# A streaming-encoder block on one core: the low part of every second v tile of the last FFN, made by ScalarE and an accumulating transfer

## The chip, the cores and the metric

The kernel runs on one core of one Trainium2 chip. A core has a matrix engine (TensorE, in the profile PE, with its weight loads as PEld), a vector engine (VectorE, DVE), an engine for functions of single elements (ScalarE, ACT), a general one (GpSimd, POOL) and a queue that issues transfers (SyncE, SP). Each works through its own list of instructions in order; they meet through semaphores. 16 DMA engines move data between the device's memory (HBM) and the on-chip memory (SBUF); TensorE adds up its products in the eight banks of PSUM. The metric is the device time of one execution in microseconds (us), lower is better.

## The reference

One layer over 256 rows of 2048 numbers: a half-step FFN, a mixer (mLSTM heads beside recurrent channels), and a second half-step FFN, each with a normalisation that is shifted and scaled by a condition c. The change lies in the second FFN:

```python
def _swiglu(u, w13, w2):
    g, v = jnp.split(u @ w13, 2, axis=-1)
    return (jax.nn.silu(g) * v) @ w2
...
        y = _swiglu(modulate(x, 2), ffn2_w13[l], ffn2_w2[l])
        x = _layer_norm(ALPHA * x + FFN_WEIGHT * gate[:, 2, None, :] * y, ln_g[l, 2], ln_b[l, 2])
```

`u` is 256 x 2048, `w13` is 2048 x 11264 (5632 columns of g, 5632 of v), `w2` is 5632 x 2048; everything is float32.

## The kernel before

**Two parts for every number.** The products run in a float32 form of TensorE (`F32R`, fp32r in the profile) that keeps fewer digits than float32. So each weight tile is split into a high part (the value, written as fp32r) and a low part (the value minus the high part), and the activations `u` likewise (`uh`, `ul`). A product is then three matmuls: activation high by weight high (L271), activation high by weight low (L272), activation low by weight high (L273). These are the three lines of `mov_t`; `mov_w` calls it once for each half of the 256 rows.

**A weight tile's way.** `load` takes a raw buffer, one of four, and lets SyncE fetch a tile of 128 x 2048 numbers, 1024 KB (L87). `split` takes a `hi` and a `lo` buffer, three of each in rotation; ScalarE writes `hi` (L97), then VectorE writes `lo` as raw minus hi (L99), which also releases the raw buffer. `load_w` is the two together. The four raw buffers also serve "ada" tiles: weights of the condition, which VectorE reduces beside the FFN's work at a fixed rate (`tick`, L191).

**The last FFN.** `ffn(2, ...)` has no `start`. Its 5632 inner columns are worked in 11 blocks of 512. `rows_block` computes one block: four g tiles (k = 0 to 3), each a fourth of the 2048 inner elements, into two banks (one for each half of the rows), then four v tiles into two others; then `swiglu` makes silu(g) * v. Block 0 is begun ahead of the FFN and goes through `met`; the other ten take the path shown. Their results are transposed by TensorE (`turn_one`, L685), after the g tiles k = 1 and 2 of the next block or within the w2 products, and split by ScalarE (hth, L687) and VectorE (htl, L688). After every two blocks, `g2` multiplies the 16 w2 tiles of the group before (rw, lw, hw in the profile; banks py). In the profile the g tiles of all FFNs are rfg, hfg and lfg, with the products fg, and the v tiles rfv, hfv and lfv, with the products fv. `closing` and `boundary` finish the last group and the normalisation.

**Order.** The program is written in order of use, and a planner places the instructions on their engines by a simulated timeline. The tiles' buffers rotate, so a cast (L97) can start once TensorE is done with the tile three places back in the rotation.

Of the kernel before, what the change touches and what calls it, by code (L numbers as in the profile page):

```python
# [11 lines left out]
F32 = mybir.dt.float32  # L12
F32R = mybir.dt.float32r
AF = mybir.ActivationFunctionType
ALU = mybir.AluOpType

P = 128
# [30 lines left out]
def block_kernel(ctx: ExitStack, tc: tile.TileContext, a: dict, out: bass.AP):  # L48
    nc = tc.nc
    cst = ctx.enter_context(tc.tile_pool(name="cst", bufs=1))  # L50
    big = ctx.enter_context(tc.tile_pool(name="big", bufs=1))
    wp = ctx.enter_context(tc.tile_pool(name="wp", bufs=1))
# [12 lines left out]
    def bank(name):  # L65
        return psp.tile([P, 512], F32, tag="ps", name=name)
# [4 lines left out]
    def raw_tile(name):  # L71
        n_raw[0] += wide[0]
        if wide[0] and n_raw[0] % 3 == 0:
            return slot(name)[:, 0:D]
        return wp.tile([P, 2048], F32, tag="raw", bufs=4, name=name)
# [7 lines left out]
    def load(src, name, into=None):  # L83

        tick()
        raw = raw_tile("r" + name)
        queue().dma_start(raw, src)  # L87
        return raw, name, into

    def split(tile, act, low):  # L90

        raw, name, into = tile
        hi, lo = into() if into else [wp.tile([P, 2048], F32R, tag=w, bufs=3, name=w[0] + name) for w in ("hi", "lo")]
        step = 512 if fine[0] else 2048
        cols = [slice(c, c + step) for c in range(0, 2048, step)]
        for w in cols:
            act.copy(cut(hi, w), like(raw[:, w], hi))  # L97
        for w in cols:
            low.tensor_sub(cut(lo, w), like(raw[:, w], lo), cut(hi, w).bitcast(F32))  # L99
        return hi, lo  # L100

    def load_w(src, name, into=None):

        return split(load(src, name, into), nc.scalar, nc.vector)

    def cut(t, w):

        return t[:, w] if len(t.shape) == 2 else t[:, w.start // P:w.stop // P, :]

    def like(ap, t):  # L110
        return ap if len(t.shape) == 2 else ap.rearrange("p (a b) -> p a b", b=P)
# [17 lines left out]
    def queue():  # L129

        return Q if wide[0] else nc.sync
# [38 lines left out]
    uh, ul = u2[:, :, 0, :], u2[:, :, 1, :]  # L170
# [28 lines left out]
    def tick():  # L199

        credit[0] += credit[1]
        while todo and credit[0] >= 1.0:
            credit[0] -= 1.0
            ada_tile(V if wide[0] else nc.vector)
# [59 lines left out]
    def mov_t(ps, hl, acth, actl, k0, t, first, last):  # L264

        hi, lo = hl
        tk = slice(t * P, (t + 1) * P)
        for j in range(4):
            w = slice(j * 512, (j + 1) * 512)
            o = like(ps, hi)  # L270
            nc.tensor.matmul(o, acth[:, k0 + j, tk], cut(hi, w), start=first and j == 0, stop=False)  # L271
            nc.tensor.matmul(o, acth[:, k0 + j, tk], cut(lo, w), start=False, stop=False)  # L272
            end = nc.tensor.matmul(o, actl[:, k0 + j, tk], cut(hi, w), start=False, stop=last and j == 3)  # L273
        return end
# [21 lines left out]
    def mov_w(pss, hl, acth, actl, k0, first, last):  # L296
        for t in range(NT):
            end = mov_t(pss[t], hl, acth, actl, k0, t, first, last)
        return end
# [30 lines left out]
    def boundary(s, ps, hls, order, mm, sts, following, gated=False):  # L330
# [152 lines left out]
        for k in ready:  # L483
            fw[k] = split(fw[k], nc.scalar, V)
# [132 lines left out]
    def met(passed, src, nm):  # L617

        _, ps, hl, raws = passed
        pss = [ps, bank(f"{nm}b1")]  # L620
        alone = [k for k in range(4) if k not in raws]
        for k in range(4):
            if k:
                hl = split((raws[k], f"{nm}b{k}", None), nc.scalar, nc.vector) if k in raws else load_w(src[k], f"{nm}b{k}")
            if k in alone:
                mov_t(pss[0], hl, uh, ul, k * 4, 0, not raws and k == 0, k == alone[-1])
            mov_t(pss[1], hl, uh, ul, k * 4, 1, k == 0, k == 3)
        return pss
# [4 lines left out]
    def ffn(s, w13, w2, start, following=None):  # L633
# [11 lines left out]
        def new_h(gi):  # L645
            hts[gi] = [slot(f"{w}{gi}", F32R)[:, 0:GRP * S].rearrange("p (a b) -> p a b", a=GRP) for w in ("hth", "htl")]

        def rows_block(b, passed=None):

            i = 8 * (b - b0)  # L650
            if passed:
                pg, pv = passed[0], met(passed, w13[4:8], f"fv{s}")
            else:
                pg = [bank(f"fg{s}{b}{t}") for t in range(NT)]
                for k in range(4):
                    end = mov_w(pg, load_w(w13[i + k], f"fg{s}_{b}{k}"), uh, ul, k * 4, k == 0, k == 3)
                    if k in (1, 2):
                        turn_one(end)
                pv = [bank(f"fv{s}{b}{t}") for t in range(NT)]
                for k in range(4):  # L660
                    mov_w(pv, load_w(w13[i + 4 + k], f"fv{s}_{b}{k}"), uh, ul, k * 4, k == 0, k == 3)
            if 4 * b // GRP not in hts:
                new_h(4 * b // GRP)
            for t in range(NT):
                swiglu(b, t, pg[t], pv[t])

        def swiglu(b, t, g, v):

            sg = sm.tile([P, 512], F32, tag="u", bufs=2, name=f"sg{s}{b}{t}")
            nc.scalar.activation(sg, g, AF.Silu)  # L670
            nc.vector.tensor_mul(sg, sg, v)
            to_turn.append((b, t, sg))

        def turn_one(end):

            if not to_turn:
                return
            b, t, sg = to_turn.pop(0)
            hth, htl = hts[4 * b // GRP]
            i = 4 * b % GRP  # L680
            tk = slice(t * P, (t + 1) * P)
            ps = bank(f"th{b}{t}")
            with tc.issue_after(end.ins):
                for j in range(4):
                    nc.tensor.transpose(ps[:, j * P:(j + 1) * P], sg[:, j * P:(j + 1) * P], ident)  # L685
            ps = ps.rearrange("p (a b) -> p a b", a=4)
            nc.scalar.copy(hth[:, i:i + 4, tk], ps)  # L687
            nc.vector.tensor_sub(htl[:, i:i + 4, tk], ps, hth[:, i:i + 4, tk].bitcast(F32))  # L688
            if to_make:
                swiglu(*to_make.pop(0))  # L690
# [152 lines left out]
        def g1(gi):  # L843
            grp = groups[gi]
            if start and gi == 2:
                new_h(gi)
                with tc.issue_after(evac[-1].ins):
                    nc.scalar.dma_start(bq, a["b_s"])
                    nc.scalar.dma_start(rgp, a["rgp"])
                to_make.extend((b, t, part[b, 0][t], part[b, 1][t]) for b in (4, 5) for t in range(NT))  # L850
                for t in range(NT):
                    swiglu(*to_make.pop(0))
                return
            if start and gi == 3:
                for t in range(NT):
                    nc.scalar.dma_start(x[:, t, :], a["x"][t * P:(t + 1) * P, :])
                scale_x()
            for b in range(grp[0] // 4, grp[-1] // 4 + 1):
                if b or start:
                    rows_block(b)  # L860
# [73 lines left out]
        if start is not None:  # L934
            ramp(start)
            credit[:] = 0.0, FFN1_RATE
            done = 2
            g2(0)
        else:
            credit[:] = -2.0, FFN2_RATE  # L940
            rows_block(0, nxt.pop())
# [482 lines left out]
```

## Time and profile before

| | |
|---|---|
| median of two runs | 1896.52 us (1895.68 to 1897.36) |
| the profiled execution, first to last instruction | 1893.8 us |
| TensorE, mean granted clock | 0.999 of full speed |
| weight tiles of 128 x 2048 in the last FFN's ten regular blocks | 80, of them 40 v tiles |
| one cast of such a tile on ScalarE (L97, hfv) | 1.91 us |
| one subtraction of such a tile on VectorE (L99, lfv) | 2.29 us |
| one load of such a tile, issue to landing (rfv) | 4.8 us |

How to read the lines that follow. A row of the timeline has the start in us from the span's start, the duration in us, the engine, the line of the kernel, the operation, and what it writes and reads; in brackets stands how long the engine had been idle, and what ended that. A row of a tile's view groups equal instructions: their count behind the x, then the least, median and largest duration in ns, then the first and last start. A row of windows has the stretch, its length, the busy time of each engine with its number of instructions, the clock granted to TensorE, the share of the DMA engines' time in use and the rate. "DMA to landing" is the time from the start of the issuing instruction to the data's arrival, least, median and largest.

### The profile page before, as it was taken

The numbers are of one execution on the slowest core, as the hardware profiler recorded it, in microseconds if no ns is written. First come the engines' busy times: TensorE is split into PE (matmuls) and PEld (weight loads), VectorE is DVE, ScalarE is ACT, GpSimd is POOL, SyncE is SP. The second block draws the span as 40 slices with busy tenths as digits, with TensorE's granted clock in tenths as the row PEclk, the third lists the DMA queues.
The fourth block names the chain that finished last, engine by engine and source line by source line (L and its number), as shares of the span: only waits on it lengthen the run. The fifth ranks groups of instructions, "written<-read, shape, count | busy, mean of one in ns | idle before, by whom it ended". The sixth has DMA issues, their size and how long they took to land.

```text
span 1893.8 us, 21255 instructions
## 1 busy us (share of the span) xinstructions
PE 1880.4 (99%) x8591; PEld 1544.5 (82%) x8591; DVE 1411.9 (75%) x1372; ACT 831.2 (44%) x790; POOL 41.3 (2%) x65
## 2 busy tenths in 40 slices
PE   9999999999999999999999999999999999999998
PEld 6788888888888888788888887888888888888886
DVE  6899998887887977798986877556555644545666
ACT  4443444533334335756643357343434334343341
POOL 0000000000000000000000121000000000000000
PEclk9999999999999999999999999999999999999999
DMA  9989889899899886477787663666676655555562
GB/s 378 416 355 360 311 315 374 336 354 351 344 362 356 333 316 252 170 289 269 274 320 269 215 248 128 242 257 248 239 258 242 227 196 193 184 200 202 198 222 89
DMA packets 74498, 515.87 MB, mean 272 GB/s; under 512 B 8688, under 2 KB 8864, under 8 KB 13472
## 3 DMA queue, kind: packets, MB, share of 16 engines
q1 hardware_dynamic: 72144, 507.54, 71.3%
q10 hardware_dynamic: 1728, 3.80, 0.6%
q0 software_dynamic: 528, 3.17, 0.4%
q8 instruction: 67, 1.10, 0.2%
q14 instruction: 31, 0.25, 0.0%
HBM read 512.36 MB, written 2.12 MB: 272 GB/s over the span
## 4 chain that ended last, share of the span: by engine, by line
PE 94%; DVE 3%; DMA 1%; ACT 1%; issue 1%; POOL 0%; POOLq 0%; DVEq 0%; SPq 0%; ACTq 0%
PE py L272 6%; PE py L271 6%; PE py L273 6%; PE fg L272 6%; PE fg L271 6%; PE fg L273 6%; PE fv L271 6%; PE fv L272 6%; PE fv L273 6%; PE pj L260 5%; PE pj L262 3%; PE tl L271 2%; PE tl L272 2%; PE tl L273 2%; PE rv L738 2%; PE rv L739 2%
## 5 line engine op out<-in xcount | busy, mean ns | idle before, releaser
L191 DVE CUSTOM_DVE_ANT_0 ada<-ada,scb,badac 128x2048 f32<-128x2048 f32 x110 | 258.0, 2346 | 11.3 <-DMA ada<-in_w_ada 10.9
L99 DVE TENSOR_TENSOR lw<-rw,hw 128x2048 fp32r<-128x2048 f32 x81 | 185.3, 2290 | 96.2 <-ACT hw L97 96.2
L97 ACT CAST hw<-rw 128x2048 fp32r<-128x2048 f32 x81 | 155.1, 1914 | 216.9 <-PE py L273 80.8
L99 DVE TENSOR_TENSOR lfv<-rfv,hfv 128x2048 fp32r<-128x2048 f32 x60 | 137.5, 2292 | 133.9 <-ACT hfv L97 133.7
L99 DVE TENSOR_TENSOR lfg<-rfg,hfg 128x2048 fp32r<-128x2048 f32 x60 | 137.5, 2291 | 89.7 <-ACT hfg L97 89.6
L272 PE MATMUL py<-lw,hth 128*128 128x512 f32 x512 | 199.4, 389 | 0.1
L273 PE MATMUL py<-hw,htl 128*128 128x512 f32 x512 | 199.4, 389 | 0.0
L97 ACT CAST hfg<-rfg 128x2048 fp32r<-128x2048 f32 x60 | 114.9, 1914 | 191.4 <-PE fv L273 52.9
L271 PE MATMUL py<-hw,hth 128*128 128x512 f32 x512 | 197.7, 392 | 0.0
L97 ACT CAST hfv<-rfv 128x2048 fp32r<-128x2048 f32 x60 | 114.6, 1912 | 165.3 <-PE fg L273 91.7
L272 PE MATMUL fg<-lfg,u 128*128 128x512 f32 x480 | 187.0, 389 | 0.1
L273 PE MATMUL fg<-hfg,u 128*128 128x512 f32 x480 | 187.0, 389 | 0.0
L272 PE MATMUL fv<-lfv,u 128*128 128x512 f32 x480 | 186.8, 389 | 0.0
L273 PE MATMUL fv<-hfv,u 128*128 128x512 f32 x480 | 186.7, 389 | 0.0
L271 PE MATMUL fg<-hfg,u 128*128 128x512 f32 x480 | 185.0, 392 | 0.0
L271 PE MATMUL fv<-hfv,u 128*128 128x512 f32 x480 | 183.5, 389 | 0.0
L260 PE MATMUL pj<-u,hs 128*128 128x512 f32 x512 | 122.5, 391 | 0.0
L97 ACT CAST hra<-rra 128x2048 fp32r<-128x2048 f32 x38 | 72.6, 1915 | 102.8 <-DMA rra<-in_w_r 49.1
L272 PEld LDWEIGHTS py<-lw,hth 128*128 128x128 f32 x512 | 96.2, 188 | 20.4 <-DVE lw L99 0.9
L273 PEld LDWEIGHTS py<-hw,htl 128*128 128x128 f32 x512 | 96.1, 188 | 20.2
L271 PEld LDWEIGHTS py<-hw,hth 128*128 128x128 f32 x512 | 95.9, 188 | 19.3
L260 PEld LDWEIGHTS pj<-u,hs 128*128 128x128 f32 x512 | 94.3, 188 | 18.4
(472 smaller groups left out, 3552.5 us busy)
## 6 DMA issues: line engine op xcount, KB each, us to landing
ada<-in_w_ada SPq DMA_DIRECT2D x138, 1024.0 KB, 6.0
rw<-in_w SPq DMA_DIRECT2D x81, 1024.0 KB, 5.0
rfg<-in_w SPq DMA_DIRECT2D x60, 1024.0 KB, 4.8
rfv<-in_w SPq DMA_DIRECT2D x60, 1024.0 KB, 4.8
rra<-in_w_r SPq DMA_DIRECT2D x45, 1024.0 KB, 7.4
rs<-in_w_s SPq DMA_DIRECT2D x32, 1024.0 KB, 4.9
rwo<-in_w_out SPq DMA_DIRECT2D x16, 1024.0 KB, 4.8
rv<-in_w_vo SPq DMA_DIRECT2D x8, 1024.0 KB, 4.9
```

The lines of the kernel that those rows point to most:

```text
L97: act.copy(cut(hi, w), like(raw[:, w], hi))
L99: low.tensor_sub(cut(lo, w), like(raw[:, w], lo), cut(hi, w).bitcast(F32))
L191: vec.tensor_tensor_reduce(raw[:, c], raw[:, c], scb[:, c], 1.0, base, ALU.mult, ALU.add, to)
L260: nc.tensor.matmul(ps, hi[:, k * P:(k + 1) * P], both(k), start=k == 0, stop=False)
L262: nc.tensor.matmul(ps[:, 0:S], lo[:, k * P:(k + 1) * P], uh[:, k, :], start=False, stop=k == KT - 1)
L271: nc.tensor.matmul(o, acth[:, k0 + j, tk], cut(hi, w), start=first and j == 0, stop=False)
L272: nc.tensor.matmul(o, acth[:, k0 + j, tk], cut(lo, w), start=False, stop=False)
L273: end = nc.tensor.matmul(o, actl[:, k0 + j, tk], cut(hi, w), start=False, stop=last and j == 3)
L738: pe.matmul(pss[t], uh[:, k0 + j, tk], hi[:, w], start=go, stop=False)
L739: pe.matmul(pss[t], uh[:, k0 + j, tk], lo[:, w], start=False, stop=False)
```

## The change

A second form of the split, `split_moved`, is added. ScalarE writes `hi` as before, in one piece. ScalarE then writes `lo` as minus one times `hi`, and GpSimd issues a transfer that adds the raw tile to `lo`, which then holds raw minus hi. VectorE takes no part. `rows_block` uses it in the last FFN (`not start`) for the v tiles k = 1 and 3; the v tiles k = 0 and 2, and all g and w2 tiles, go through `split` as before, and so does everything in the first FFN.

```diff
@@ -97,6 +97,15 @@
+        return hi, lo
+
+    def split_moved(tile):
+
+        raw, name, _ = tile
+        hi, lo = [wp.tile([P, 2048], F32R, tag=w, bufs=3, name=w[0] + name) for w in ("hi", "lo")]
+        nc.scalar.copy(hi, raw)
+        nc.scalar.mul(lo, hi.bitcast(F32), -1.0)
+        nc.gpsimd.dma_start(lo, raw, accum_op=ALU.add)
         return hi, lo
 
@@ -658,7 +667,10 @@
                 pv = [bank(f"fv{s}{b}{t}") for t in range(NT)]
                 for k in range(4):
-                    mov_w(pv, load_w(w13[i + 4 + k], f"fv{s}_{b}{k}"), uh, ul, k * 4, k == 0, k == 3)
+                    tile = load(w13[i + 4 + k], f"fv{s}_{b}{k}")
+                    moved = not start and k % 2
+                    mov_w(pv, split_moved(tile) if moved else split(tile, nc.scalar, nc.vector),
+                          uh, ul, k * 4, k == 0, k == 3)
```

## The prediction

> **What bounds the kernel now.** I read the head of the profile first, then the busy time of the engines in the stretch that holds the last FFN.
>
> ```profile
> span 1893.8 us, 21255 instructions
> PE 1880.4 (99%) x8591; PEld 1544.5 (82%) x8591; DVE 1411.9 (75%) x1372; ACT 831.2 (44%) x790; POOL 41.3 (2%) x65
> ...
> core 0: us, PE busy (x), PEclk, DMA share, GB/s
> 1200.00:1880.00 680.00, 680.00 (x3044) 1.00 0.58 213
> ...
> core 0: us, PE busy (x) PEld busy (x) DVE busy (x) ACT busy (x) POOL busy (x), PEclk, DMA share, GB/s
> 1300.00:1730.00 430.00, 430.00 (x1925) 356.11 (x1924) 231.31 (x144) 170.51 (x117) 0.00 (x0) 1.00 0.60 217
> ```
>
> TensorE is busy 99% of the span. From 1200 to 1880 us, where every edited tile lies, it is busy 680.00 of 680.00 us, at a granted clock of 1.00. In most of that stage VectorE works 231 of 430 us, ScalarE 171 and GpSimd nothing. So nothing here waits for VectorE in the end: taking work from it gives nothing, and the only question is whether the new way delivers the low part before TensorE wants it. The profiled span is 1893.8 us; the runs have a median of 1896.5, and I add the difference of 2.7 at the end.
>
> **How much time a tile has.** Next I read one block of the last FFN in order of time, ScalarE and then TensorE.
>
> ```profile
> 1304.13 1.91 ACT L97 CAST hfv<-rfv 128x2048 fp32r<-128x2048 f32 x1 [3.52 <-PE fg L273]
> 1305.95 0.58 ACT L687 CAST hth<-th 128x512 fp32r<-128x512 f32 x1
> 1307.32 0.60 ACT L670 ACTIVATE sg<-fg 128x512 f32<-128x512 f32 x1 [0.79 <-PE fg L273]
> 1310.04 1.91 ACT L97 CAST hfv<-rfv 128x2048 fp32r<-128x2048 f32 x1 [2.12 <-PE fg L273]
> ...
> 1315.48 1.91 ACT L97 CAST hfv<-rfv 128x2048 fp32r<-128x2048 f32 x1 [3.04 <-PE fv L273]
> 1320.92 1.91 ACT L97 CAST hw<-rw 128x2048 fp32r<-128x2048 f32 x1 [3.53 <-PE fv L273]
> 1326.36 1.91 ACT L97 CAST hw<-rw 128x2048 fp32r<-128x2048 f32 x1 [3.53 <-PE fv L273]
> ...
> 1309.84 0.39 PE L271 MATMUL fv<-hfv,u 128*128 128x512 f32 x1
> ...
> 1315.28 0.39 PE L271 MATMUL fv<-hfv,u 128*128 128x512 f32 x1
> 1315.50 0.39 PE L272 MATMUL fv<-lfv,u 128*128 128x512 f32 x1
> ...
> 1326.38 0.39 PE L272 MATMUL fv<-lfv,u 128*128 128x512 f32 x1
> ```
>
> The v half of this block starts at 1309.84, and its second tile (k = 1, an edited one) 5.44 us later, at 1315.28. The product that first needs its low part (L272) starts at 1315.50. Its high part was begun at 1304.13, at the moment when TensorE let go of the tile two places ahead (the idle time before the cast ended with PE fg L273). Three buffers of each kind thus give every tile some 11.4 us, from the buffer's release to the use. The fourth v tile (k = 3) is cast at 1315.48 and wanted at 1326.38, 10.9 us.
>
> **The change part by part.**
>
> ```profile
> L97 ACT CAST hfv<-rfv x40: 1895/1913/1915, 1209.3 to 1800.9; 128x2048 fp32r<-128x2048 f32 x40
> L99 DVE TENSOR_TENSOR lfv<-rfv,hfv x40: 2292/2293/2293, 1211.3 to 1802.8; 128x2048 fp32r<-128x2048 f32 x40
> ```
>
> The last FFN has 40 such v tiles, in ten blocks (the first block goes through another function and keeps its form). Of these, k = 1 and k = 3 change: 20 tiles.
>
> Removed: 20 VectorE subtractions of 2.293 us, 45.9 us, all beside TensorE's work. Gain on the path: 0. The cover is TensorE's unbroken 680 us; nothing is late without them.
>
> Added on ScalarE: 20 writes of the negated high part. No row shows this operation; the cast of the same shape takes 1.91 us, and I take that: 38 us in all, beside 171 of 430 us busy. Behind it wait, for k = 1, an hth copy of 0.58 us and an sg of 0.60, which come at most 1.9 us late; TensorE is then occupied with v tiles for 21.8 us more, and I cost the delay at 0. For k = 3 ScalarE sits idle until 1320.92. Successive casts start 1.82 us apart where they abut (1304.13 to 1305.95), so the negation ends at about 1307.9, or 1308.4 if the hth copy goes first; for k = 3 at 1319.2. From there the transfer has 1315.5 - 1308.1 = 7.4 us until TensorE needs it, and for k = 3 1326.4 - 1319.2 = 7.2 us.
>
> Added on GpSimd's queue: 20 transfers of 1024 KB, SBUF to SBUF, adding to their target. The trace has no accumulating transfer. The nearest rows are the transfers on this same queue for the gate: 8 KB into DRAM, then 1024 KB into SBUF.
>
> ```profile
> L212 POOL DMA_DIRECT2D rowd<-grow x1: 618/618/618, 1731.4 to 1731.4; - x1
> ...
> DMA to landing us min/median/max: 1.7/1.7/1.7
> L213 POOL DMA_DIRECT2D gate<-rowd x1: 563/563/563, 1733.7 to 1733.7; - x1
> ...
> DMA to landing us min/median/max: 6.8/6.8/6.8
> L213 POOL DMA_DIRECT2D gate<-rowd x1: 570/570/570, 591.4 to 591.4; - x1
> ...
> DMA to landing us min/median/max: 10.2/10.2/10.2
> 591.40:601.60 10.20, 10.20 (x47) 8.45 (x46) 6.92 (x6) 3.61 (x2) 0.57 (x1) 1.00 1.01 414
> 1733.70:1740.50 6.80, 6.80 (x34) 5.65 (x33) 3.27 (x3) 2.29 (x2) 0.56 (x1) 1.00 0.85 325
> ```
>
> In the stage of the change, among its loads, 1024 KB land 6.8 us after the issue and 8 KB after 1.7: a fixed part of about 1.7 and a moving part of 5.1 us. Where the DMA engines were full (share 1.01), 1024 KB took 10.2. An accumulating transfer moves more than a plain one: it reads the raw tile, reads the low tile too, and writes the sum. Lower end: the second reading hides beside the first, 6.8 us. Upper end: two passes (1.7 + 2 x moving part) with a moving part halfway between 5.1 and 10.2 - 1.7 = 8.5, so 6.8: 1.7 + 13.6 = 15.3 us. I take two passes at this stage's own moving part, since the 6.8 us row comes from among these very loads: 1.7 + 2 x 5.1 = 11.9 us. An estimate, and the one number on which all hangs.
>
> The Trainium skill ("Collectives: The Full Stack", Part 3, on ReduceScatter against AllGather) says that a DMA add is slow for its second source read, not for the addition, and gives a measured ratio of 1.93. By that ratio the landing would be 1.7 + 1.93 x 5.1 = 11.5 us and the sum below about 5 us smaller; no row here shows an adding transfer.
>
> New wait on TensorE: at k = 1 it waits 11.9 - 7.4 = 4.5 us. At k = 3 the wait doesn't come again in full: that tile's buffers are those of v tile 0, free at 1315.5, ahead of the wait. Its work runs on during the wait, and TensorE comes to it 4.5 us later: 11.9 - 7.2 - 4.5 = 0.2. What is behind TensorE in its own queue all waits with it, since the products of one v group follow one another in the same bank. The next block starts level again, as the head start is counted in tiles.
>
> Moved in time: the raw buffer is released by the landing, about 1308.1 + 11.9 = 1320.0, and no longer by a subtraction that ends at about 1308.3; SyncE's loads wait for just such releases.
>
> ```profile
> SPq L87 <- DVE lfv L99: 136.5, 28, 5.5
> ...
> DMA to landing us min/median/max: 4.7/4.8/6.3
> ```
>
> The 28 such waits come to 136.5 us already, with no idle TensorE. The load that follows into this buffer lands at about 1320.0 + 4.8 = 1324.8; the tile four places on is cast at 1326.36 (plus the 4.5 that TensorE lost). 1.6 us to spare or more, and beyond that what such a tile's own head start leaves, 11.4 - 1.9 - 2.3 = 7.2 us; cost 0. If an ada tile takes the next place in the rotation, the margin is 1320.92 + 4.5 - 1324.8 = 0.6 and then the same 7.2.
>
> GpSimd's queue is empty in the stage (x0 above), so 0.56 us of issue delays nobody; the two gate transfers of this stage lie at 1731, after nine of ten blocks, and go ahead of the last. DMA engines: 217 GB/s at a share of 0.60 is 362 GB/s when full, 2.9 us for 1024 KB; 20 tiles at two passes add 116 us to a share of 0.58 over 680 us, so about 0.75: not full on average.
>
> Sum: ten blocks x (4.5 + 0.2) = 47 us. 1893.8 + 47 + 2.7 = 1943.5; I say 1943 us, 2.5% slower.
>
> **The rivals.** *The transfer is hidden* (ends on the other side). If reading the target overlaps with reading the source, it lands between the plain 6.8 us and 11.9. Up to 7.2 us there is no wait at all: 1896.5. Two per cent of 1896.5 are 38 us, 3.8 us a block, which is about what a measurement of this kernel can tell from no change; so up to a landing of 11.1 us, 0.8 under my estimate, it counts as no change. For it: the row of 6.8 us. Against: one tile more has to be read, over engines already at 0.60. In the middle of this case, at 9 us, the time is 1896.5 + 10 x 1.6 = 1913.
>
> *The transfer is slower than two passes.* At 15.3 us: 7.9 us at k = 1; the second transfer is issued at 1319.2 while the first still runs to 1323.4, and if it loses half of these 4.2 us, k = 3 waits 15.3 + 2.1 - 7.2 - 7.9 = 2.3. Ten blocks: 102 us, 1998. For it: the 10.2 us row, and that the target's type (fp32r) is not the source's (f32), which no transfer here shows. Against: on average the engines don't fill.
>
> *Writing the descriptors waits for VectorE.* One subtraction is the most that could stand in front: 11.9 + 2.3 = 14.2 us, 10 x 2.3 more: 1966. For it: the slow gate transfer (10.2) had VectorE busy 6.92 us, the fast one 3.27. Against: the DMA share explains that as well, and both issues took 0.56 to 0.57. The Trainium skill ("SBUF — State Buffer", the box on the DVE-blocks-DMA trap) has this rule, for VectorE instructions in two-port modes, and says tensor_tensor has none; the matching issue times agree as far as they go.
>
> *No gain is left over.* That VectorE's freed time makes it faster has no place to come from: 0.00 us of TensorE idle time in 680.
>
> **How the numbers follow.** Landing between 11.1 and 13.2 us, the forecast: 0.42, with a range of its own from 1935 to 1957 (10 x 5.8 = 58, plus overlap). Hidden wholly or in part, up to 11.1 us: 0.40, of which 0.12 at no cost. Slower than two passes 0.12, waiting for VectorE 0.05. Faster 0.01. So slower 0.59, same 0.40, faster 0.01. The range for 8 in 10 reaches from just about no cost to the two-pass bound: 1897 to 1997.
>
> **What would show it.** Right: L272 of fv waits at k = 1 on the transfer in ten blocks, some 4 to 5 us each, and k = 3 hardly at all; the new POOL issue group lands at about 12 us; ScalarE +38, VectorE -46 us; TensorE busy as before and the span longer by the waits alone. Wrong: a landing under 7 us, waits at k = 3 as long as at k = 1 (then 20 x 4.5 = 90 us, 1987), or SyncE's loads arriving late, with waits of fg tiles on their casts.

## The result, and the profile after

The changed kernel takes 1922.96 us (median of two runs, 1922.58 to 1923.34) against 1896.52: a ratio of 1.0142, with an interval of 1.0112 to 1.0171. It is slower, by 26 us, and less so than the 1943 us that were forecast. The loss stays under the 2% (38 us) from which on the prediction called a kernel slower, so the outcome is the one that it gave 0.40, not the one that it gave 0.59.

The head of the profile after, with the row of the new transfer from its list of DMA issues:

```profile
span 1920.8 us, 21312 instructions
PE 1888.0 (98%) x8591; PEld 1544.2 (80%) x8591; DVE 1367.6 (71%) x1352; ACT 867.2 (45%) x810; POOL 58.0 (3%) x85
...
lfv<-rfv POOLq DMA_DIRECT2D x20, 1024.0 KB, 8.6
```

VectorE is busy 44 us less and ScalarE 36 us more, as counted before (46 and 38). The span is 27.0 us longer, and TensorE is no longer without a gap. The windows over the last FFN, and who waited for whom there, both of the kernel after:

```profile
core 0: us, PE busy (x) PEld busy (x) DVE busy (x) ACT busy (x) POOL busy (x), PEclk, DMA share, GB/s
1200.00:1880.00 680.00, 661.39 (x2927) 542.01 (x2926) 326.07 (x231) 295.80 (x194) 18.17 (x22) 0.99 0.72 242
```

```profile
PEld fv L281 <- DMA lfv<-rfv: 24.5, 16, 3.4
PE fv L281 <- DMA lfv<-rfv: 18.2, 13, 3.0
```

L281 is the old L272, the first product that reads the low part. It waits for the transfer and, but for 0.4 us in the closing tiles, TensorE waits for nothing else. The matmul row counts a wait from the modelled end of the matmul before, which is somewhat too late, the weight-load row (PEld) from the end of the last load, which is somewhat too early; so the waits are between 18.2 and 24.5 us of the 27.0. A count that needs neither: in these 680 us TensorE began 2927 matmuls, 3044 before, and 117 fewer at 680 / 3044 = 0.223 us each are 26.1 us. What the waits don't hold of it is mostly a clock that falls after some of them (below).

The low tile's own view, after:

```profile
L99 DVE TENSOR_TENSOR lfv<-rfv,hfv x20: 2287/2293/2293, 1211.6 to 1821.5; 128x2048 fp32r<-128x2048 f32 x20
L107 ACT ACTIVATE lfv<-hfv x20: 1899/1917/1924, 1217.9 to 1826.9; 128x2048 fp32r<-128x2048 f32 x20
L108 POOL DMA_DIRECT2D lfv<-rfv x20: 833/846/965, 1220.1 to 1829.1; - x20
...
DMA to landing us min/median/max: 6.9/8.6/13.2
```

The negation takes 1.92 us, as the cast's row had suggested. A transfer lands 6.9 us after its issue at the least, 8.6 in the median, 13.2 at the most. Where that comes from is seen in one block, the one whose rows stood in the prediction. The timelines of ScalarE, GpSimd, SyncE and TensorE, after:

```profile
1307.51 1.91 ACT L106 CAST hfv<-rfv 128x2048 fp32r<-128x2048 f32 x1 [3.51 <-PE fg L282]
1309.32 0.57 ACT L699 CAST hth<-th 128x512 fp32r<-128x512 f32 x1
1309.79 1.92 ACT L107 ACTIVATE lfv<-hfv 128x2048 fp32r<-128x2048 f32 x1
...
1312.01 0.84 POOL L108 DMA_DIRECT2D lfv<-rfv  x1 [34.62 <-DVE htl L700]
1322.99 0.84 POOL L108 DMA_DIRECT2D lfv<-rfv  x1 [10.13 <-ACT lfv L107]
...
1322.06 0.33 SPq L87 DMA_DIRECT2D rw<-in_w  x1
1322.49 0.37 SPq L196 DMA_DIRECT2D ada<-in_w_ada  x1
...
1322.05 0.50 PE L281 MATMUL fv<-lfv,u 128*128 128x512 f32 x1 [2.78 <-DMA lfv<-rfv]
...
1336.21 0.50 PE L281 MATMUL fv<-lfv,u 128*128 128x512 f32 x1 [0.91 <-DMA lfv<-rfv]
```

Follow it in order. The hth copy goes ahead of the negation, the transfer of tile 1 is issued at 1312.01 and lands 10.0 us later, and TensorE's first product with it starts at 1322.05, after 2.78 us of idle time. In the next 0.5 us two loads leave SyncE, an rw and an ada tile: the first had waited for the raw buffer that the transfer had been reading, the second stood behind it in SyncE's queue. At 1322.99, behind them, the transfer of tile 3 is issued. It takes 13.2 us, and TensorE waits again.

### The profile page after: what moved, and what is told of

Read it like the earlier page. It is cut to its first block, busy times and chain, and to the rows that moved or that the text cites. A ratio compares the mean times of both kernels' runs of the same rounds, so it can differ in the third digit from the quotient of the medians.

```text
span 1920.8 us, 21312 instructions
## 1 busy us (share of the span) xinstructions
PE 1888.0 (98%) x8591; PEld 1544.2 (80%) x8591; DVE 1367.6 (71%) x1352; ACT 867.2 (45%) x810; POOL 58.0 (3%) x85
## 5 line engine op out<-in xcount | busy, mean ns | idle before, releaser
L97 ACT CAST hw<-rw 128x2048 fp32r<-128x2048 f32 x81 | 155.0, 1913 | 228.7 <-PE py L282 74.5
L281 PE MATMUL fv<-lfv,u 128*128 128x512 f32 x480 | 190.0, 396 | 18.2 <-DMA lfv<-rfv 18.2
L281 PE MATMUL py<-lw,hth 128*128 128x512 f32 x512 | 199.4, 389 | 0.1
L281 PE MATMUL fg<-lfg,u 128*128 128x512 f32 x480 | 187.1, 390 | 0.1
L99 DVE TENSOR_TENSOR lfv<-rfv,hfv 128x2048 fp32r<-128x2048 f32 x40 | 91.7, 2291 | 92.0 <-ACT hfv L97 92.0
L281 PEld LDWEIGHTS fv<-lfv,u 128*128 128x128 f32 x480 | 90.9, 189 | 43.4 <-DMA lfv<-rfv 24.5
L97 ACT CAST hfv<-rfv 128x2048 fp32r<-128x2048 f32 x40 | 76.4, 1912 | 91.4 <-PE fg L282 47.0
L281 PEld LDWEIGHTS py<-lw,hth 128*128 128x128 f32 x512 | 96.2, 188 | 20.5 <-DVE lw L99 0.9
```

## The experiments

All are edits of the changed kernel unless said otherwise; each ratio is to the kernel before, run on the same chip. "Theory A" came from the traces before and after: all of the loss is a low part that lands after TensorE wants it, and the landing depends on which loads stand in line ahead of the transfer. (The expectations call the loss 27 us, from the profiled spans; by the medians it is 26.4.)

### Without the transfer

```diff
-        nc.gpsimd.dma_start(lo, raw, accum_op=ALU.add)
```

> Leaves out the addition: the low part of the 20 tiles stays minus the high part, so ScalarE's negation and the missing VectorE subtraction are left alone. Theory A (all of the loss is the transfer: its landing against a head start of 7.2 to 7.4 us): 1896, within 3 us of the kernel before. Rival (a part of the loss is ScalarE's 38 us of new work, which delays what is queued behind it): 1900 to 1910, with TensorE idle time at casts.

1895.85 us, ratio 1.0003 (0.9993 to 1.0012). This kernel leaves out the addition, so its low parts are not raw minus hi. Taking 46 us off VectorE gains nothing, and 38 us more on ScalarE cost nothing. All of the loss is the transfer's.

### A plain copy in place of the adding one

```diff
-        nc.gpsimd.dma_start(lo, raw, accum_op=ALU.add)
+        nc.gpsimd.dma_start(lo, raw)
```

> Leaves out the addition: the transfer writes the raw tile over the low part instead of adding it. Everything else as in the changed kernel, the wait for the landing too. Theory A (an adding packet holds a DMA engine twice as long as a plain one, 0.63 against 0.31 us for 8 KB): the landing falls by some 2.5 us, from a median of 8.6 to about 6, under the head start nearly everywhere: 1896 to 1901. Rival (the landing is set by waiting in line and by the writing of descriptors, not by the adding): median landing stays above 8, 1912 or more.

1895.70 us, ratio 1.0000 (0.9990 to 1.0009). The landings:

```profile
DMA to landing us min/median/max: 4.1/4.3/6.1
```

The median fell by 4.3 us, more than the 2.5 expected, and no landing is above the head start. It is the adding that makes the transfer late.

### Only tile 1, only tile 3

```diff
-                    moved = not start and k % 2
+                    moved = not start and k == 1
```

(and `k == 3` in the other kernel.)

> Only v tile 1 of the ten blocks is changed (10 tiles). Theory A (waits of the changed kernel's k = 1 tiles stay, about 11 us in sum, some less because no k = 3 transfer holds back loads): 1902 to 1908. Rival B (each place has its own slowness, nothing carries over from one tile to the next): 1907 or 1908.

> Only v tile 3 of the ten blocks is changed (10 tiles). Theory A (k = 3 lands late, 8.2 to 13.2 us, because the k = 1 transfer two tiles ahead kept its raw buffer, so that two loads were issued together just ahead of it): without k = 1 it lands in 7 to 8.5 us; 1897 to 1906. Rival B (k = 3 is slow by its own place): landings stay at a mean of 10, and since TensorE is no longer held up at k = 1 each wait is the whole 3 us: 1920 to 1926.

1903.44 us, ratio 1.0041 (1.0026 to 1.0056), and 1904.04 us, ratio 1.0045 (1.0030 to 1.0060). Alone, each costs about 8 us (7.6 and 8.2); together they cost 26.4, some 10 more than the sum. The low tile's landings, first with tile 1 alone, then with tile 3 alone:

```profile
DMA to landing us min/median/max: 6.9/7.0/9.2
```

```profile
DMA to landing us min/median/max: 6.9/7.0/10.5
```

Tile 3 is not slow by its place: with no transfer two tiles ahead of it, its median is that of tile 1. This was the prediction that told theory A from its rival, and the rival (1920 or more) is out.

The starts of the transfers' 8 KB packets in the traces show the line itself. In these two kernels the first packet starts 1.4 to 1.5 us after the issue, all 20 times. In the changed kernel tile 3's starts 2.4 to 5.0 us after it, all ten times, with 1.0 to 1.7 MB of SyncE's loads moved in between. The two transfers don't meet each other: each one of tile 1 had landed before that of tile 3 was issued.

The waits that are left with one tile alone have other causes, which theory A doesn't name. In five of the matmul's seven waits, loads that began after the transfer's first packet moved 0.4 to 1.0 MB beside it. In the other two no load ran. One of them, with tile 1 alone, is the transfer issued at 1665.68, which landed after 9.2 us; the DMA view from 1672.7 to 1674.9, its last 2.2 us:

```profile
q8 instruction: 1, 0.02, 2.8%
q0 software_dynamic: 1, 0.00, 0.1%
```

All but one of its 144 packets were through by 1672.7. The last one, a few bytes, came after a packet of 16 KB on the queue that the profile calls instruction. The other of the two, and the wait of 1.99 us at 1689.50 in the changed kernel, have such a packet too and no load.

The kernel with tile 1 alone also shows the price of adding by itself. The DMA views of one undisturbed transfer, with tile 1 alone (a window of 7.0 us) and with the plain copy (4.2 us); a row has the queue, its packets, MB, and their time as a share of the 16 engines' window:

```profile
q0 software_dynamic: 144, 1.05, 74.1%
```

```profile
q0 software_dynamic: 144, 1.05, 64.8%
```

The same 144 packets hold the engines for 0.741 x 7.0 = 5.2 us when they add and 0.648 x 4.2 = 2.7 us when they copy: 1.9 times as long. The Trainium skill's ratio of 1.93 ("Collectives: The Full Stack", Part 3) agrees.

### The low buffer first

```diff
-        nc.scalar.copy(hi, raw)
-        nc.scalar.mul(lo, hi.bitcast(F32), -1.0)
+        nc.scalar.mul(lo, raw, -1.0)
         nc.gpsimd.dma_start(lo, raw, accum_op=ALU.add)
+        nc.scalar.copy(hi, raw)
```

> ScalarE writes the low buffer first, as minus one times the raw tile (rounded the same way), and the high part after it, so the transfer is issued some 1.9 us earlier; all else as in the changed kernel. Theory A (wait = landing minus head start): the head start grows from about 7 to 9 us, the plain landings of 6.9 to 7.0 are hidden with 2 us to spare and only those above 9 still show; raw buffers are freed earlier too: a loss of 2 to 10 us, 1898 to 1906. Rival (TensorE loses by the DMA engines' load as such, whenever the transfer starts): 1918 or more, as in the changed kernel.

1912.85 us, ratio 1.0090 (1.0075 to 1.0105). A miss for both: 10 us come back, not 17 or more. The landings are still 6.9 to 12.8 us with a median of 8.3, so the line ahead of tile 3 had not become shorter; the 2 us more of head start hide the plain landings, but not those. Of the 8.7 us that the matmul still waits, 8.2 are at tile 3.

### From HBM, and both

```diff
-        nc.gpsimd.dma_start(lo, raw, accum_op=ALU.add)
+        nc.gpsimd.dma_start(lo, src, accum_op=ALU.add)
...
-                    mov_w(pv, split_moved(tile) if moved else split(tile, nc.scalar, nc.vector),
+                    mov_w(pv, split_moved(tile, w13[i + 4 + k]) if moved else split(tile, nc.scalar, nc.vector),
```

> The transfer adds the weight tile straight from HBM and not from the raw buffer, which ScalarE's cast then releases at once; 20 MB more are read from HBM. Theory A (the two tiles together cost 27 and not 8 + 8 us because the transfer keeps the raw buffer, loads pile up behind it and stand in line ahead of the next transfer): no loads are held, k = 3 lands as k = 1 does, near 7 us: 1903 to 1911. Rival (the excess comes from one transfer meeting the other, or from too many bytes for the DMA engines): 1918 or more.

> Both of the two edits: the low buffer written first, and the transfer from HBM. Theory A: head start about 9 us, landings near 7, no load held: 1895 to 1899, no wait left. Rival of the DMA engines' load: 1910 or more.

1922.73 us, ratio 1.0139 (1.0122 to 1.0156), and 1912.76 us, ratio 1.0088 (1.0073 to 1.0103). Theory A missed both times, and the time alone would speak for the rival. The landings of the first, then of both edits, and the matmul's waits of the first show something else:

```profile
DMA to landing us min/median/max: 8.0/8.8/10.9
```

```profile
DMA to landing us min/median/max: 9.1/9.4/13.0
```

```profile
1275.60 0.50 PE L281 MATMUL fv<-lfv,u 128*128 128x512 f32 x1 [2.61 <-DMA lfv<-in_w]
1325.22 0.80 PE L281 MATMUL fv<-lfv,u 128*128 128x512 f32 x1 [3.22 <-DMA lfv<-in_w]
1417.83 0.50 PE L281 MATMUL fv<-lfv,u 128*128 128x512 f32 x1 [1.63 <-DMA lfv<-in_w]
1466.28 0.50 PE L281 MATMUL fv<-lfv,u 128*128 128x512 f32 x1 [3.70 <-DMA lfv<-in_w]
```

These are four blocks in a row, one wait each, all at tile 1. Added up over the ten blocks from such rows, the matmul's waits come to 17.2 us at tile 1 and 1.8 at tile 3, where the changed kernel had 8.1 and 10.1. With no raw buffer held, tile 3's landings are only 0.3 us longer than tile 1's (means of 9.2 and 8.9 us), where the changed kernel had 10.2 and 7.9. That much is as theory A said; that tile 3 hardly waits owes something to tile 1's longer waits too, which bring TensorE to it later. But no transfer lands quickly any more. The DMA view of one of the quickest, from 1594.55 to 1602.50:

```profile
q0 software_dynamic: 144, 1.05, 72.9%
q1 hardware_dynamic: 125, 0.89, 29.1%
```

The transfer holds the engines for 0.729 x 7.95 = 5.8 us, not much over the 5.2 from the raw buffer, and SyncE's loads for 2.3 us more. At least 0.8 MB of loads move between issue and landing of every one of the 20 transfers, where the quick ones of the changed kernel had none: the cast frees the raw buffer as soon as it ends (18 of SyncE's waits in this kernel end with it), and the next load goes out just ahead of the transfer. With both edits it is 0.9 MB or more. So the line got shorter at tile 3 and longer at tile 1, and the time doesn't settle the mechanism. What HBM as a source costs by itself these runs don't show; the 8 KB packets take 629 ns in the median in this kernel and in the changed one.

### Adding transfers that nobody waits for

```diff
+    apart = [dr2.tile([P, 2048], F32, name=f"apart{i}") for i in range(2)]
+    n_held = [0]
...
         nc.scalar.copy(hi, raw)
-        nc.scalar.mul(lo, hi.bitcast(F32), -1.0)
-        nc.gpsimd.dma_start(lo, raw, accum_op=ALU.add)
+        nc.vector.tensor_sub(lo, raw, hi.bitcast(F32))
+        n_held[0] += 1
+        nc.gpsimd.dma_start(apart[n_held[0] % 2], raw, accum_op=ALU.add)
```

> The kernel before, with VectorE's subtraction for all tiles, and beside it for the same 20 tiles an adding transfer of the raw tile into a scratch tensor in HBM that nothing reads (two such tensors, filled once at the start of the last FFN). The raw buffer is held as in the changed kernel and the DMA engines do as much adding, but no product waits for it. Theory A (held buffers and late loads cost nothing by themselves, only a low part that lands late does): 1896 to 1898. Rival (late loads stop TensorE by themselves): 1903 or more, with waits of casts on loads.

1895.78 us, ratio 1.0000 (0.9991 to 1.0009). TensorE's windows there:

```profile
1200.00:1850.00 650.00, 650.00 (x2912) 1.00 0.77 252
```

The DMA engines' share is 0.77, above the 0.72 of the changed kernel over nearly the same stretch, and TensorE has no idle time. But the edit does less than was expected of it. What GpSimd waited for ahead of these transfers, and SyncE's wait for them:

```profile
  DMA rfv<-in_w: 582.9, 20
...
SPq L87 <- DMA apart<-rfv: 33.1, 13, 7.7
```

A transfer here needs only the raw tile, so it was issued when that had landed, ahead of the split, and in 17 of 20 tiles it landed before VectorE's subtraction ended. The raw buffers were hardly held longer than in the kernel before. So 20 adding transfers and a busier DMA cost nothing where no product waits for them; that held buffers cost nothing is not shown by this kernel.

### Low buffer first, only tile 1

```diff
-        nc.scalar.copy(hi, raw)
-        nc.scalar.mul(lo, hi.bitcast(F32), -1.0)
+        nc.scalar.mul(lo, raw, -1.0)
         nc.gpsimd.dma_start(lo, raw, accum_op=ALU.add)
+        nc.scalar.copy(hi, raw)
...
-                    moved = not start and k % 2
+                    moved = not start and k == 1
```

> The low buffer written first, and only v tile 1 of the ten blocks changed. Theory A (wait = landing minus head start, landing = time in line behind loads + 5.2 us of packets + about 1.7): nothing is in line, landings near 7, at most 9.2, against a head start of about 9: 1895 to 1898, no wait. Rival (an adding transfer costs TensorE some 0.8 us each however early it starts): 1903, as with only v tile 1 changed in the order of the changed kernel.

1896.63 us, ratio 1.0003 (0.9994 to 1.0013), where the other order cost 8 us. The transfers still take 6.9 us or more, but start 2 us earlier, and one wait of 0.5 us is left. This is the clean case of wait = landing minus head start.

### Twenty tiles, four apart

```diff
-                    end = mov_w(pg, load_w(w13[i + k], f"fg{s}_{b}{k}"), uh, ul, k * 4, k == 0, k == 3)
+                    tile = load(w13[i + k], f"fg{s}_{b}{k}")
+                    moved = not start and k == 1
+                    end = mov_w(pg, split_moved(tile) if moved else split(tile, nc.scalar, nc.vector),
+                                uh, ul, k * 4, k == 0, k == 3)
...
-                    moved = not start and k % 2
+                    moved = not start and k == 1
```

> 20 tiles changed as in the changed kernel, but four tiles apart instead of two: tile 1 of g and tile 1 of v in each of the ten blocks. Theory A (what makes 27 us of 8 + 8 is loads held back by one transfer that stand in line ahead of the next, two tiles later): four tiles apart the line is worked off, landings at a median of 7 to 7.5: 1905 to 1913. Rival (20 adding transfers cost what 20 cost, wherever they lie): 1920 to 1925.

> The same 20 tiles, four apart, with the low buffer written first. Theory A: landings near 7 against a head start of about 9: 1895 to 1900, as many tiles moved off VectorE as in the changed kernel at next to no cost; not faster than the kernel before, since TensorE had no idle time there. Rival (20 cost what 20 cost): about 1912, as with the low buffer first and tiles two apart.

1913.90 us, ratio 1.0095 (1.0080 to 1.0110): 18 us for 20 tiles, against 26 for 20 tiles two apart. That is just beyond the range written down for theory A (1905 to 1913) and well short of the rival's. Landings of the v tiles and of the g tiles:

```profile
DMA to landing us min/median/max: 6.9/7.1/9.1
```

```profile
DMA to landing us min/median/max: 6.9/7.0/9.8
```

The medians are those of a transfer alone. With the low buffer first the same tiles take 1902.58 us, ratio 1.0031 (1.0020 to 1.0042): the rival's 1912 is out, but theory A's 1900 was too low. The ten runs go from 1897.6 to 1907.0. The profiled one has a span of 1895.8 us, 2 us above that of before, and so lies at the quick end; what makes the others longer isn't seen in it and stays open.

None of these kernels beats the one before, and theory A has no place from which one could: there was no idle time to win. A fourth buffer of each kind was not tried.

## Why the prediction was right, and where not

**TensorE is the bound, VectorE's relief is worth nothing, ScalarE's work lies under cover.** Right on all three counts: 1895.85 us without the transfer.

**Two passes for an adding transfer.** Right at the packets: 1.9 times a copy's engine time. (Put into the prediction's sum, the ratio of 1.93 takes 4 us off it, not the 5 that stand there: 4.1 + 0.2 us in ten blocks are 43.)

**The moving part of a pass, 5.1 us.** Wrong, and the largest error of the sum. A pass moves for 2.7 us. The gate transfer's 6.8 us were split into 1.7 fixed and 5.1 moving by means of a small transfer; but much of the 5.1 was time in line. The DMA view of the first 3.5 us after that transfer's issue at 1733.70, in the kernel before, has loads and no packet of it:

```profile
q1 hardware_dynamic: 116, 0.95, 75.5%
```

Its data moved in the other 3.3 us, and a plain copy on the same queue lands in 4.3. Doubling all of the 5.1 gave 11.9 us; an adding transfer alone lands in 6.9 to 7.0 (the plain copy's 4.3 plus 2.7, one pass more). The mechanism was right and this term was too big: the wait at tile 1 was put at 4.5 us in each of ten blocks, and the matmul shows 8.1 us in all ten together.

**The head start, 7.4 us at tile 1.** A little too long. GpSimd issued the transfer at 1312.01 where I had the negation end at 1307.9 to 1308.4 in a block that ran 3.4 us earlier (casts at 1304.13 and 1307.51): 0.2 to 0.7 us later, of which 0.3 is the way from ScalarE to GpSimd. So even the plain landing of 6.9 us only just arrives. (The buffers of v tile 1 come from the g tile three places back, not two, as the prediction has it; the time that it read off is right.)

**Tile 3 hardly waits (0.2 us), and the raw buffer's late release costs 0.** This step failed. It was right for what it looked at, the casts that late loads might stop. After the change the loads did come later, but one cast of the last FFN waits for one, and TensorE's waits are for the low part:

```profile
ACT hw L97 <- DMA rw<-in_w: 5.4, 1, 5.4
```

But it looked at the loads' arrival only, not at what they would stand ahead of. The tile's own view for another block, and the DMA view of the first 5 us after its issue, both of the kernel after:

```profile
L108 POOL DMA_DIRECT2D lfv<-rfv x1: 842/842/842, 1276.5 to 1276.5; - x1
...
DMA to landing us min/median/max: 11.9/11.9/11.9
```

```profile
q1 hardware_dynamic: 223, 1.70, 100.3%
```

For 5 us after the issue the engines move 1.70 MB of SyncE's loads and no packet of the transfer: it stands behind loads that the transfer of tile 1 had held back. This low part still came just in time, as TensorE had itself waited 1.70 us at tile 1. In the block followed above it was too late; from the issue at 1322.99 to 1327.60 there is again no packet of the transfer:

```profile
q1 hardware_dynamic: 179, 1.34, 93.7%
```

SyncE's waits have a row that wasn't there before:

```profile
SPq L87 <- DMA lfv<-rfv: 180.1, 18, 14.1
```

So tile 3 cost 10.1 us of the matmul's waits, more than tile 1, though TensorE had come to it later. By the runs, having the two transfers two tiles apart is worth 26.4 - 7.6 - 8.2 = 10.6 us. The two errors have opposite signs: the sum of 47 us was too high for the landing and too low for the line. That it came as near as it did is partly luck: of 45 us forecast at tile 1 the matmul shows 8.1, and about half of the loss lies in terms that stood at 2 us (tile 3, 10.1) or were not in the sum (the clock, below). Of the prediction's own signs of being wrong, the waits at tile 3 as long as at tile 1 came true.

**The rivals.** The one that came nearest was the transfer partly hidden, given 0.40: a landing below 11.1 us in most blocks, and a time within 2%. The slow landings of the second rival (13.2 us at most) occur too, in a few tiles, by the mechanism named there, full engines. That writing the descriptors waits for VectorE finds no support in the late tiles: in the 11.9 us above it was the loads' packets that ran.

**What no step had: the clock.** The windows of TensorE, each 1 us, around the wait at 1322.05, after:

```profile
1320.00:1321.00 1.00, 0.00 (x0) 1.00 0.53 107
1321.00:1322.00 1.00, 0.00 (x0) 1.00 0.05 8
1322.00:1323.00 1.00, 0.95 (x3) 0.73 0.00 0
1323.00:1324.00 1.00, 1.00 (x3) 0.50 0.94 131
1324.00:1325.00 1.00, 1.00 (x4) 0.50 0.93 393
1325.00:1326.00 1.00, 1.00 (x4) 0.56 1.05 418
1326.00:1327.00 1.00, 1.00 (x6) 1.00 0.91 254
```

The PEclk column falls from 1.00 to 0.50 within 1322 to 1323 and is back at 1.00 by 1326, some 3.4 us; three to four matmuls fall into a window there, and six once the clock is back. The lost clock adds 0.27 + 0.50 + 0.50 + 0.44 = 1.7 us to a wait of 2.78. It happens twice, here and after the wait of 2.97 us at 1608.95: about 3.4 us, which with the 18.2 to 24.5 us of waits makes 21.6 to 27.9, and the 26.1 lost us of the matmul count lie in that. The Trainium skill ("TensorE: Matmul & The Clock Gate", Part 1) states half rate after an idle window of about 3.4 us and again about 3.4 us of work until full rate; the second agrees, and for the first waits of 2.8 to 3.0 us were enough here. They are not always enough: with tile 3 alone the clock stayed at 1.00 after a wait of 2.96 us, and in the changed kernel after one of 1.99.

## What to carry to other kernels

Work moved from an engine that has slack to a transfer is judged by one difference: landing minus head start. Measure the landing for that kind of transfer (an adding one held the engines 1.9 times as long as a copy), and take a row's time in line apart from its moving part before scaling it. And ask what the transfer keeps: the buffer it reads is released late, the loads behind it come out together, and they stand in line ahead of the next transfer; starting it as early as its data allow and spacing such transfers, both together, left 7 of the 26 us here.

## What the hardware did that was not expected

- A transfer issued just behind 1 to 2 loads on another queue did not share the engines with them at once: for 5 us the loads had 100.3% of the engines' time and the transfer none.
- A transfer with no load beside it landed after 9.2 us and not 6.9: the last of its 144 packets came behind one packet of 16 KB on the instruction queue.
- Issuing an adding transfer took GpSimd 0.85 us, the gate's plain one 0.56.
- Waits of under 3 us halved TensorE's clock for some 3.4 us, which added 1.7 us each time, in the changed kernel after 2.78 and 2.97 us; with tile 3 alone a wait of 2.96 us did not.
